# A two-layer decoder trunk: every projection computed token-major, rotation by tokens, turns by DMA, the projections in a new order

## Chip, cores and metric

The kernel runs on one core of one Trainium2 chip. The metric is the device time of one execution in microseconds (us), lower is better: the median of three runs of the kernel before is 318.63 us (317.89 to 319.02). The profile is of one more execution, which took 318.17 us, of which 316.0 us lie between its first and its last instruction (the span).

## What is computed

There are 256 tokens, 1024 features and two layers. A layer normalises `x`, projects it with one weight of 1024 x 4096, and splits the result into eight groups of 512 columns, each of four heads of 128. Four groups (RQ, RK, RV, RZ) feed a retention, four (MQ, MK, MV, MZ) an attention whose 256-token block is its own block, so that it is plain causal attention with a bias table.

```python
h = rms_norm(x, norm_g[i])
rq, rk, rv, rz, mq, mk, mv, mz = jnp.split(h @ w_in[i], cuts, axis=-1)
r_out = retention(rotary(heads(rq)), rotary(heads(rk)), heads(rv), ret_norm_g[i])
r_out = silu(rz) * r_out
m_out = moba(rms_norm(heads(mq), q_g), rms_norm(heads(mk), k_g), heads(mv), rel_bias)
m_out = silu(mz) * m_out
x = x + concatenate([r_out, m_out]) @ w_out[i]
gate = sigmoid(rms_norm(x) @ w_ple_gate[i])
x = x + gate * rms_norm(p[i] @ w_ple[i], ple_norm_g[i])
```

`rotary` turns each pair (x1, x2) of the two halves of a head by an angle that depends on the token. `retention` scores queries against keys, multiplies by a decay table, applies the result to the values, and normalises each head.

## The kernel before

**Weights.** Each group's weight comes in two stages of 1 MB (`wst`, four buffers), each of two pieces of 128 x 1024. ACT rounds a piece to a high part (`wh`, L137) and DVE computes the low part (`wl`, L138), six buffers each, so the pieces of a stage are made at most three stages ahead of TensorE (PE). A product in full precision is three matmuls: high by high, low by high, high by low (`mm3`, L146 to L148).

**Token-major and turned projections.** `project(g)` keeps 128 tokens of the activation stationary and streams 512 weight columns: 8 slices of features x 2 token halves x 3 products, 48 matmuls of 512 columns. The result has tokens on the partitions. MQ, MK, MV, RV and RZ are made this way. MZ, RQ and RK are turned: the weights are stationary and the 256 tokens stream, so that the result has the features of a head on the partitions. `project_turned_pairs` (MZ, L488 to L492) uses 96 matmuls of 256 columns, `project_turned` (RQ, RK, L469 and L470) 32 pairs of one of 512 and one of 256 columns.

**What follows a projection.** MQ and MK are normalised per head (`qk_norm`), repacked by ACT into two planes of 16 bits (`halves`, L255), turned by a DMA on SP's queue (`turned_by_dma`, L262) and copied back to `T` by DVE (L265, two copies for 128 tokens). RQ and RK are already turned: `rope` works on a head at a time, with the halves swapped by two ACT copies (L508, L509) and four DVE instructions (L507, L510, L511, L512), reading cosine and sine rows from `cst`. `gate_turned` needs the tokens' scale as a row, which `spread` and `gather` make by a small DRAM round trip. The attention's scores are made in three pieces (`moba_scores`, L546), each followed later by a softmax on DVE and ACT, a division, and a transpose on PE (`turn`, L250). `moba_out` multiplies turned values with turned probabilities (L586, L587). `ret_scores` (four), `ret_out` (two, L577) and `ret_gate` do the same for retention.

**What sets the order.** PE and SP run in the order in which the code is written; DVE and ACT are ordered by a scheduler, and then each engine works its queue in order. `project` and the turned forms call `tick()` after each sixth matmul or each head, and `later(n, f)` puts `f` into the program n ticks on. So the short groups of matmuls stand between the projections' matmuls at places given by a tick count. `ahead()` puts the next weight load into SP's queue when a stage is used, and DMA turns stand in the same queue where their tick falls. A PE result lies in one of four `acc` buffers (projections) or four `mix` buffers (short groups).

```python
ORDER = (MQ, MK, MV, MZ, RQ, RK, RV, RZ)
later(14, lambda: moba_scores(0, 0, 4))
later(15, lambda: moba_scores(1, 0, 2))
later(16, lambda: moba_scores(1, 2, 2))
project_turned_pairs(MZ, lambda h, ps: gate_turned(MZ, h, ps))
project_turned(RQ, lambda h, ps: rope(RQ, h, ps))
project_turned(RK, lambda h, ps: rope(RK, h, ps))
```

Of the kernel before, what the change touches and what calls it, by code (L numbers as in the profile page):

```python
# [24 lines left out]
H = 4  # L25
# [9 lines left out]
ORDER = (MQ, MK, MV, MZ, RQ, RK, RV, RZ)  # L35
# [6 lines left out]
C_COS, C_SIN = 0, S  # L42
C_DEC = 2 * S
# [12 lines left out]
def tile_hybrid_trunk(ctx: ExitStack, tc: tile.TileContext, first, rest, x, pT, ple_g, rel_bias,  # L56
# [42 lines left out]
    def job(key, fn):  # L99
        jobs.append((key, fn))  # L100
# [80 lines left out]
    cos, sin = cst[:, C_COS:C_COS + S], cst[:, C_SIN:C_SIN + S]  # L181
# [157 lines left out]
    for l in range(DEPTH):  # L339
        for g in ORDER:  # L340
            for half in range(2):
                if l == 0 and g == MQ:
                    first_blocks(half)
                else:
                    stage(("in", l, g, half), w_in[l, g, half])
                if l == 0 and g == RQ and half:
                    job(None, lambda: nc.sync.dma_start(cst, consts))
            if l == 0 and g == MK:
                for m in range(MT):
                    job(None, lambda m=m: nc.sync.dma_start(x_t[:, m], x[:, m]))  # L350
                shifts = bias_table()
            if l == 0 and g == MV:
# [12 lines left out]
    for l in range(DEPTH):  # L365
        rstd, hr, rstd2, epsx = [], [], [], []
        hrs = sm.tile([P, 32], F32, name="hr", bufs=2)
        nc.vector.memset(hrs, 0.0)

        def x_stats():  # L370
            for m in range(MT):
# [12 lines left out]
                h = hrs[:, m:m + 1]  # L384
# [6 lines left out]
            nc.vector.transpose(hrt, hrs)  # L391

        hd = dram.tile([MT, P], F32, name=f"hd{l}")
        hrow = big.tile([P, S], F32, name="hrow", bufs=1)

        hrt = sm.tile([P, 32], F32, name="hrt", bufs=1)

        def spread():

            for m in range(MT):  # L400
                nc.sync.dma_start(hd[m].rearrange("(b i) -> b i", i=32), hrt.rearrange("(b j) i -> b j i", j=32)[:, m])

        def gather():

            nc.sync.dma_start(hrow, bass.AP(tensor=hd.tensor, offset=hd.offset, ap=[[0, P], [1, S]]))
# [51 lines left out]
        def project_turned(g, use):  # L457

            ps = [acc_p.tile([P, 2, S], F32, name="acc") for _ in range(H)]
            for half in range(2):
                parts = load_w(("in", l, g, half))
                for h in range(H):
                    sl = slice(h * DH, (h + 1) * DH)
                    for k in range(4):
                        wh, wl = parts[k // 2]
                        kk, end = half * 4 + k, half == 1 and k == 3
                        nc.tensor.matmul(ps[h], wh[:, k % 2, sl], aB[:, kk], start=kk == 0, stop=False)  # L469
                        nc.tensor.matmul(ps[h][:, 0], wl[:, k % 2, sl], aB[:, kk, 0], start=False, stop=end)  # L470
                    if half:
                        with tc.high_priority(offset=PRIO):
                            use(h, ps[h])
                    tick()

        def project_turned_pairs(g, use):


            ps = [acc_p.tile([P, 2, S], F32, name="acc") for _ in range(H // 2)]
            for half in range(2):  # L480
                parts = load_w(("in", l, g, half))
                for h in range(H):
                    sl = slice(h * DH, (h + 1) * DH)
                    o = ps[h // 2][:, h % 2]
                    for k in range(4):
                        wh, wl = parts[k // 2]
                        kk, end = half * 4 + k, half == 1 and k == 3
                        nc.tensor.matmul(o, wh[:, k % 2, sl], aB[:, kk, 0], start=kk == 0 and h % 2 == 0,  # L488
                                         stop=False, skip_group_check=True)
                        nc.tensor.matmul(o, wh[:, k % 2, sl], aB[:, kk, 1], start=False, stop=False,  # L490
                                         skip_group_check=True)
                        nc.tensor.matmul(o, wl[:, k % 2, sl], aB[:, kk, 0], start=False, stop=end,  # L492
                                         skip_group_check=True)
                    if half and h % 2:
                        with tc.high_priority(offset=PRIO):
                            use(h - 1, ps[h // 2])
                    tick()

        def rope(g, h, ps):
            if h == 0:  # L500
                T[g] = big.tile([P, H, S], F32, name="T")
            dst = T[g][:, h]
            r = DH // 2
            t = tmp_p.tile([P, 2, S], F32, name="tmp")
            b = tmp_p.tile([P, S], F32, name="tmp")
# [20 lines left out]

        def gate_turned(g, h, ps):
            if h == 0:
                G[g] = big.tile([P, H, S], F32, name="G", bufs=1)
            t = tmp_p.tile([P, 2, S], F32, name="tmp")  # L530
            th = tmp_p.tile([P, 2, S], F32, name="tmp")
            nc.vector.tensor_tensor(t, ps, hrow[:, None, :].to_broadcast([P, 2, S]), op=ALU.mult)
            nc.scalar.activation(th, t, AF.Tanh)
            nc.vector.scalar_tensor_tensor(G[g][:, h:h + 2], th, 1.0, t, op0=ALU.add, op1=ALU.mult)
# [3 lines left out]
        def moba_scores(m, h0, per):  # L538
# [17 lines left out]
            ri = sm.tile([P, H], F32, name="ri")  # L556
            nc.vector.reciprocal(ri[:, :per], DEN[m][:, h0:h0 + per])
# [11 lines left out]
            later(8, turn)  # L569

        yT, yTh, yTl, _ = act_tiles()
# [9 lines left out]
        def moba_out(h0):  # L581

            ps = mix_p.tile([P, 2, S], F32, name="mix")
            for j in range(2):
                v = V[MV][:, :, (h0 + j) * DH:(h0 + j + 1) * DH]
                nc.tensor.matmul(ps[:, j], v[:, 0], PT[:, h0 + j, :S], start=True, stop=False)  # L586
                nc.tensor.matmul(ps[:, j, P:], v[:, 1], PT[:, h0 + j, S:], start=False, stop=True)  # L587
# [61 lines left out]
        later(8, spread)  # L649
        later(15, gather)  # L650
# [14 lines left out]
        for h in range(H):  # L665
            later(5 + h, lambda h=h: ret_scores(h))
# [3 lines left out]
        later(3, lambda: ret_out(0))  # L670
        later(4, lambda: ret_out(1))
# [89 lines left out]
def _constants():  # L761
# [6 lines left out]
    c[:, C_COS:C_COS + S] = np.concatenate([cos, cos], 1).T  # L768
    c[:, C_SIN:C_SIN + S] = np.concatenate([-sin, sin], 1).T
# [64 lines left out]
```

## Time and profile before

| | us | |
|---|---|---|
| median of 3 runs | 318.63 | 317.89 to 319.02 |
| the profiled execution | 318.17 | |
| its span | 316.0 | |
| PE busy | 310.0 | 98% |
| DVE busy | 243.3 | 77% |
| ACT busy | 201.0 | 64% |

Matmuls are pipelined, and the profile models their ends: a row gives 0.39 us for a matmul of 512 columns although the next one starts after 0.23 us. So what a matmul costs PE is read from the distance between starts, not from its duration. DVE's and ACT's rows have a similar, smaller overlap: three instructions of 1.22 us each in a row take 3.48 us together, some 0.07 us less than their durations for each. The first layer's eight projections run from 5 us to 123 us, the second's from 166 us to 282 us.

### The profile page before, as it was taken

What the parts mean: (1) busy time and instruction counts of PE and PEld (TensorE: products, weight loads), DVE (VectorE), ACT (ScalarE), POOL (GpSimd) and SP (SyncE); (2) the same over time, 40 slices, a digit from 0 to 9 for tenths busy, and PEclk for the clock granted to TensorE, in tenths of its full rate; (3) what the DMA queues carried; (4) which work ended last, traced back from release to release, by engine and by line L of the source; (5) the groups of instructions that cost most, each with busy time, mean ns of one, the idle gap of its engine ahead of it and who ended that gap; (6) DMA issues with size and microseconds to landing.
All of it is one profiled execution on the core that took longest, in us unless ns stands there. A gap on an engine that the chain in (4) does not pass through costs nothing.

```text
span 316.0 us, 4502 instructions
## 1 busy us (share of the span) xinstructions
PE 310.0 (98%) x1609; PEld 263.2 (83%) x1609; DVE 243.3 (77%) x444; ACT 201.0 (64%) x382; POOL 27.5 (9%) x45
## 2 busy tenths in 40 slices
PE   8999999999999999999999999999999999999994
PEld 4888899888888888888888888998888888888884
DVE  5798889679967977959698877586799669969632
ACT  5888947886842635845586987469769435547411
POOL 4015200000001100011001521000000011000000
PEclk9999999999999999999999999999999999999999
DMA  7999999444560139500997459943345530390001
GB/s 263 418 409 395 243 276 421 163 152 152 222 234 1 33 64 427 242 2 34 385 418 251 177 127 308 372 144 133 133 141 197 196 135 17 63 386 2 33 33 66
DMA packets 23350, 62.17 MB, mean 197 GB/s; under 512 B 13853, under 2 KB 14881, under 8 KB 17185
## 3 DMA queue, kind: packets, MB, share of 16 engines
q1 hardware_dynamic: 23320, 61.89, 55.5%
q8 instruction: 12, 0.20, 0.3%
q14 instruction: 10, 0.07, 0.1%
q10 hardware_dynamic: 8, 0.00, 0.0%
HBM read 57.69 MB, written 1.06 MB: 186 GB/s over the span
## 4 chain that ended last, share of the span: by engine, by line
PE 94%; ACT 2%; DVE 1%; issue 1%
PE acc L146 21%; PE acc L147 21%; PE acc L148 21%; PE acc L469 8%; PE acc L470 4%; PE acc L492 2%; PE acc L490 2%; PE acc L488 2%; PE mix L250 2%; PE mix L577 2%; PE mix L546 2%; PE mix L169 1%; PE mix L146 1%; PE mix L147 1%; PE mix L148 1%
## 5 line engine op out<-in xcount | busy, mean ns | idle before, releaser
L138 DVE TENSOR_TENSOR wl<-wst,wh 128x1024 fp32r<-128x1024 f32 x96 | 115.6, 1219 | 24.4 <-ACT wh L137 23.7
L137 ACT CAST wh<-wst 128x1024 fp32r<-128x1024 f32 x96 | 98.4, 1053 | 41.9 <-PE acc L148 25.0
L146 PE MATMUL acc<-wh,a 128*128 128x512 f32 (+1 forms) x296 | 116.2, 392 | 0.0
L148 PE MATMUL acc<-wh,a 128*128 128x512 f32 (+1 forms) x296 | 113.8, 384 | 0.0
L147 PE MATMUL acc<-wl,a 128*128 128x512 f32 (+1 forms) x296 | 113.7, 384 | 0.0
L148 PEld LDWEIGHTS acc<-wh,a 128*128 128x128 f32 x296 | 55.6, 188 | 11.2
L147 PEld LDWEIGHTS acc<-wl,a 128*128 128x128 f32 x296 | 55.7, 188 | 11.0 <-DVE wl L243 0.6
L146 PEld LDWEIGHTS acc<-wh,a 128*128 128x128 f32 x296 | 55.8, 188 | 10.7 <-ACT wh L236 0.4
L469 PE MATMUL acc<-a,wh 128*128 128x512 f32 x128 | 46.8, 407 | 0.6 <-DVE tmp L507 0.6
L470 PE MATMUL acc<-a,wl 128*128 128x256 f32 x128 | 35.9, 281 | 0.0
L469 PEld LDWEIGHTS acc<-a,wh 128*128 128x128 f32 x128 | 24.1, 188 | 6.3 <-PE mix L587 0.9
L470 PEld LDWEIGHTS acc<-a,wl 128*128 128x128 f32 x128 | 24.2, 189 | 0.1
L488 PE MATMUL acc<-a,wh 128*128 128x256 f32 x64 | 18.6, 291 | 0.0
L729 ACT ACTIVATE tmp<-acc,hr 128x512 f32<-128x512 f32 (+1 forms) x9 | 5.8, 640 | 19.4 <-PE acc L148 17.7
L492 PE MATMUL acc<-a,wl 128*128 128x256 f32 x64 | 18.1, 283 | 0.0
L490 PE MATMUL acc<-a,wh 128*128 128x256 f32 x64 | 18.1, 283 | 0.0
L159 POOL TENSOR_TENSOR ro<-rs_t,neghalf 128x4 f32<-128x4 f32 x4 | 4.0, 1006 | 142.3 <-DVE rs_t L158 142.3
L730 DVE SCALAR_TENSOR_TENSOR tmp<-tmp,E 128x512 f32<-128x512 f32 (+1 forms) x9 | 5.7, 631 | 12.7 <-ACT tmp L729 12.7
L255 ACT COPY u<-tok 128x1024 uint16<-128x1024 uint16 x12 | 12.6, 1062 | 0.3 <-DVE tok L451 0.3
L488 PEld LDWEIGHTS acc<-a,wh 128*128 128x128 f32 x64 | 12.3, 192 | 0.1
L490 PEld LDWEIGHTS acc<-a,wh 128*128 128x128 f32 x64 | 12.3, 192 | 0.1
L492 PEld LDWEIGHTS acc<-a,wl 128*128 128x128 f32 x64 | 12.2, 191 | 0.0
(121 smaller groups left out, 373.1 us busy)
## 6 DMA issues: line engine op xcount, KB each, us to landing
wst<-in_w_in SPq DMA_DIRECT2D x30, 1024.0 KB, 6.2
wst<-in_w_out SPq DMA_DIRECT2D x8, 1024.0 KB, 4.8
wst<-in_w_gate SPq DMA_DIRECT2D x8, 1024.0 KB, 6.6
wst<-in_w_ple SPq DMA_DIRECT2D x2, 1024.0 KB, 6.5
wst<-in_rest SPq DMA_DIRECT2D x4, 384.0 KB, 7.2
E<-in_rest SPq DMA_DIRECT2D x3, 384.0 KB, 3.8
x_t<-in_x SPq DMA_DIRECT2D x2, 512.0 KB
gb<-in_ple_g SPq DMA_DIRECT2D x2, 512.0 KB, 4.5
```

Of the source, the lines that this page charges most:

```text
L137: nc.scalar.copy(hi, s)
L138: nc.vector.tensor_tensor(lo, s, hi.bitcast(F32), op=ALU.subtract)
L146: nc.tensor.matmul(ps, ah[:, k], wh[:, kk], start=start, stop=False)
L147: nc.tensor.matmul(ps, ah[:, k], wl[:, kk], start=False, stop=False)
L148: nc.tensor.matmul(ps, al[:, k], wh[:, kk], start=False, stop=stop)
L250: nc.tensor.transpose(ps[:, j * P:(j + 1) * P], src[:, b * P:(b + 1) * P], ident)
L255: nc.scalar.copy(u, src.bitcast(U16).rearrange("p (n t) -> p t n", t=2))
L469: nc.tensor.matmul(ps[h], wh[:, k % 2, sl], aB[:, kk], start=kk == 0, stop=False)
L470: nc.tensor.matmul(ps[h][:, 0], wl[:, k % 2, sl], aB[:, kk, 0], start=False, stop=end)
L488: nc.tensor.matmul(o, wh[:, k % 2, sl], aB[:, kk, 0], start=kk == 0 and h % 2 == 0, stop=False, skip_group_check=True)
L490: nc.tensor.matmul(o, wh[:, k % 2, sl], aB[:, kk, 1], start=False, stop=False, skip_group_check=True)
L492: nc.tensor.matmul(o, wl[:, k % 2, sl], aB[:, kk, 0], start=False, stop=end, skip_group_check=True)
```

## The change

All eight groups use `project`, so `project_turned`, `project_turned_pairs`, `gate_turned` and the DRAM round trip go. RQ and RK are rotated with the tokens on the partitions, and their four pieces per layer then go the way of MQ and MK: repacked by ACT, turned by DMA, copied by DVE. The attention's output is made with the tokens on the partitions, divided and gated in one pass, and turned by DMA too. The order of the projections is MQ, MK, RQ, RK, MZ, MV, RV, RZ. The three scores, the three transposes, the two halves of `moba_out`, the four `ret_scores` and the two `ret_out` each stand in one place.

```diff
-ORDER = (MQ, MK, MV, MZ, RQ, RK, RV, RZ)
+ORDER = (MQ, MK, RQ, RK, MZ, MV, RV, RZ)
...
                 if l == 0 and g == RQ and half:
-                    job(None, lambda: nc.sync.dma_start(cst, consts))
+                    job(None, lambda: nc.sync.dma_start(cst[:, :C_DEC], consts[:, :C_DEC]))
+                if l == 0 and g == MZ and half:
+                    job(None, lambda: nc.sync.dma_start(cst[:, C_DEC:], consts[:, C_DEC:]))
...
-        def rope(g, h, ps):
...
-            nc.scalar.copy(b, ps[:, 1])
-            nc.vector.tensor_tensor(t[:, 0], ps[:, 0], b, op=ALU.add)
-            nc.scalar.copy(b[:r], t[r:, 0])
-            nc.scalar.copy(b[r:], t[:r, 0])
-            nc.vector.tensor_tensor(t[:, 1], t[:, 0], cos, op=ALU.mult)
-            nc.vector.tensor_tensor(b, b, sin, op=ALU.mult)
-            nc.vector.tensor_tensor(dst, t[:, 1], b, op=ALU.add)
+        def rope(g, ps):
+            for m in range(MT):
+                src = ps[m].rearrange("p (h a d) -> p h a d", h=H, a=2)
...
+                nc.vector.tensor_tensor(tv, src, cos, op=ALU.mult)
+                nc.vector.tensor_tensor(bv, src[:, :, ::-1], sin, op=ALU.mult)
+                o = tok_p.tile([P, GW], F32, name="tok")
+                nc.vector.tensor_tensor(o, t, b, op=ALU.add)
+                u = halves(o)
+                later((9 if g == RQ else 4) + m, lambda m=m, u=u: to_heads(g, m, u))
...
-            def divide():
-                for j in range(per):
-                    nc.scalar.activation(sv[:, j], sv[:, j], AF.Copy, scale=ri[:, j:j + 1])
-            later(3, divide, 0)
...
-            later(8, turn)
+            later(7, turn)
...
-        def moba_out(h0):
...
-            y = tok_p.tile([P, 2, S], F32, name="tok")
-            nc.vector.tensor_tensor(y, ps, G[MZ][:, h0:h0 + 2], op=ALU.mult)
-            hi = yTh[:, H + h0:H + h0 + 2]
-            nc.scalar.copy(hi, y)
-            nc.vector.tensor_tensor(yTl[:, H + h0:H + h0 + 2], y, hi.bitcast(F32), op=ALU.subtract)
+        def moba_out(m):
+            ps = pv(m, lambda h, m, b: PT[:, h, (m + b) * P:(m + b + 1) * P], V[MV])
+            ri = sm.tile([P, H], F32, name="ri")
+            nc.vector.reciprocal(ri, DEN[m])
+            nc.vector.tensor_scalar(ri, ri, hr[m], None, op0=ALU.mult)
+            y = tok_p.tile([P, GW], F32, name="tok")
+            for h in range(H):
+                sl = slice(h * DH, (h + 1) * DH)
+                nc.vector.scalar_tensor_tensor(y[:, sl], ps[:, sl], ri[:, h:h + 1], G[MZ][:, m, sl],
+                                               op0=ALU.mult, op1=ALU.mult)
+            u = halves(y)
+            later(3 + m, lambda: parts_by_dma(yT[m], H, u))
...
-        later(14, lambda: moba_scores(0, 0, 4))
-        later(15, lambda: moba_scores(1, 0, 2))
-        later(16, lambda: moba_scores(1, 2, 2))
+        def scores():
+            moba_scores(0, 0, 4)
+            moba_scores(1, 0, 2)
+            moba_scores(1, 2, 2)
+        later(16, scores)
+        for g in (RQ, RK):
+            ps = project(g)
+            with tc.high_priority(offset=PRIO):
+                rope(g, ps)
+        ps = project(MZ)
+        with tc.high_priority(offset=PRIO):
+            gate(MZ, ps)
         ps = project(MV)
         with tc.high_priority(offset=PRIO):
             value(MV, ps)
-        project_turned_pairs(MZ, lambda h, ps: gate_turned(MZ, h, ps))
-        later(10, lambda: moba_out(0))
-        later(11, lambda: moba_out(2))
-        project_turned(RQ, lambda h, ps: rope(RQ, h, ps))
-        project_turned(RK, lambda h, ps: rope(RK, h, ps))
-        for h in range(H):
-            later(5 + h, lambda h=h: ret_scores(h))
+        later(3, lambda: [moba_out(m) for m in range(MT)])
+        later(5, lambda: [ret_scores(h) for h in range(H)])
         ps = project(RV)
         with tc.high_priority(offset=PRIO):
             value(RV, ps)
-        later(3, lambda: ret_out(0))
-        later(4, lambda: ret_out(1))
+        later(3, lambda: [ret_out(m) for m in range(MT)])
```

Three places show how the queues change. The first is DVE in layer 0, from the last rows before the third projection's end to the first score. Before (`w_435` and `w_446` are the turned queries of MQ, `w_493` and `w_503` the turned keys of MK, `L550` adds the bias to a score):

```order
L138 TENSOR_TENSOR wl<-wst,wh 128x1024 x3
L265 COPY T<-w_435 128x4x128 x2
L138 TENSOR_TENSOR wl<-wst,wh 128x1024
L265 COPY T<-w_446 128x4x128 x2
L138 TENSOR_TENSOR wl<-wst,wh 128x1024
L265 COPY T<-w_493 128x4x128 x2
L265 COPY T<-w_503 128x4x128 x2
```

After, `w_430` and `w_441` are the queries, `w_487` and `w_497` the keys, and L452, L453 and L455 the rotation of RQ:

```order
L452 TENSOR_TENSOR tmp<-acc,cst 128x512
L453 TENSOR_TENSOR tmp<-acc,cst 128x512
L265 COPY T<-w_430 128x4x128 x2
L138 TENSOR_TENSOR wl<-wst,wh 128x1024
L452 TENSOR_TENSOR tmp<-acc,cst 128x512
L453 TENSOR_TENSOR tmp<-acc,cst 128x512
L265 COPY T<-w_441 128x4x128 x2
L455 TENSOR_TENSOR tok<-tmp 128x512
L138 TENSOR_TENSOR wl<-wst,wh 128x1024
L455 TENSOR_TENSOR tok<-tmp 128x512
L265 COPY T<-w_487 128x4x128 x2
L138 TENSOR_TENSOR wl<-wst,wh 128x1024 x2
```

(The keys' second half, `w_497`, follows, and then the rotation of RK.) The copies of the queries and keys now stand behind and between the six instructions that rotate RQ, which wait for RQ's last matmuls.

The second place is SP's queue from the middle of layer 0's projections on. Before, behind the turned keys of MK (`w_493`, `w_503`), only loads stand there:

```order
L405 DMA hrow<-hd_141 128x256
L262 DMA_TRANSPOSE w_493<-u_400 128x8x128
L262 DMA_TRANSPOSE w_503<-u_414 128x8x128
L347 DMA cst<-in_consts 128x1536
L125 DMA wst<-in_w_in 128x2048 x6
L125 DMA wst<-in_w_out 128x2048 x4
L330 DMA pf<-in_pT 128x512
```

After, `u_507` and `u_515` are the repacked RQ, `u_627` and `u_635` RK, `u_866` and `u_885` the attention's output; the loads on both sides of `w_703` are those of RV's second stage and of RZ:

```order
L349 DMA cst<-in_consts 128x1024
L125 DMA wst<-in_w_in 128x2048 x3
L262 DMA_TRANSPOSE w_656<-u_507 128x8x128
L262 DMA_TRANSPOSE w_666<-u_515 128x8x128
L262 DMA_TRANSPOSE w_683<-u_627 128x8x128
L125 DMA wst<-in_w_in 128x2048
L262 DMA_TRANSPOSE w_703<-u_635 128x8x128
L125 DMA wst<-in_w_in 128x2048 x2
L125 DMA wst<-in_w_out 128x2048 x2
L262 DMA_TRANSPOSE w_937<-u_866 128x8x128
L262 DMA_TRANSPOSE w_950<-u_885 128x8x128
L125 DMA wst<-in_w_out 128x2048 x2
```

Six turns now stand among the weight loads, and a load behind a turn is issued only when ACT has made what the turn reads.

The third place is ACT in layer 1 of the changed kernel, at the end of MV (`u_2124` is the second half of RK, `L462` makes the values, `u_2355` and `u_2374` are the attention's output):

```order
L255 COPY u_2124<-tok 128x1024
L137 CAST wh<-wst 128x1024 x3
L462 ACTIVATE V<-acc,rstd 128x512 x2
L137 CAST wh<-wst 128x1024 x2
L255 COPY u_2355<-tok 128x1024
L255 COPY u_2374<-tok 128x1024
```

The third of the three casts ahead of the values is the first piece of RZ's weight, so the values stand behind that weight's load.

## Rows read from the trace of the kernel before

**Rows 1.** The page: busy time by engine, and the granted clock by slice.
```profile
PE 310.0 (98%) x1609; PEld 263.2 (83%) x1609; DVE 243.3 (77%) x444; ACT 201.0 (64%) x382; POOL 27.5 (9%) x45
...
PEclk9999999999999999999999999999999999999999
```

**Rows 2.** The page: the chain that ended last, by engine.
```profile
PE 94%; ACT 2%; DVE 1%; issue 1%
```

**Rows 3.** Timeline of PE: start, duration, instruction; MZ's, RQ's and RZ's projections.
```profile
38.22 0.28 PE L488 MATMUL acc<-a,wh 128*128 128x256 f32 x1
...
46.86 1.06 PE L546 MATMUL mix<-T 128*128 128x128 f32 x8
...
52.70 0.39 PE L469 MATMUL acc<-a,wh 128*128 128x512 f32 x1
...
58.71 0.40 PE L469 MATMUL acc<-a,wh 128*128 128x512 f32 x1
...
101.10 0.48 PE L146 MATMUL acc<-wh,a 128*128 128x512 f32 x1
...
122.96 0.27 PE L250 MATMUL mix<-ident,x_t 128*128 128x128 f32 x1
```

**Rows 4.** Timeline of PE: where it waits, in brackets what it waited for.
```profile
68.86 0.39 PE L587 MATMUL mix<-PS,V 128*128 128x128 f32 x2
69.54 0.47 PE L469 MATMUL acc<-a,wh 128*128 128x512 f32 x1 [0.29 <-DVE tmp L507]
```

**Rows 5.** Timeline of PE: short groups and the projection's matmuls behind them.
```profile
67.78 0.59 PE L586 MATMUL mix<-PS,V 128*128 128x256 f32 x2
68.20 0.39 PE L587 MATMUL mix<-PS,V 128*128 128x128 f32 x2
...
97.13 1.05 PE L577 MATMUL mix<-V,PS 128*128 128x128 f32 x8
97.94 0.48 PE L146 MATMUL acc<-wh,a 128*128 128x512 f32 x1
98.25 0.40 PE L147 MATMUL acc<-wl,a 128*128 128x512 f32 x1
...
99.40 1.95 PE L577 MATMUL mix<-V,PS 128*128 128x128 f32 x16
```

**Rows 6.** Groups by line and shape: count | busy us, mean ns | idle before, releaser.
```profile
L138 DVE TENSOR_TENSOR wl<-wst,wh 128x1024 fp32r<-128x1024 f32 x96 | 115.6, 1219 | 24.4 <-ACT wh L137 23.7
L137 ACT CAST wh<-wst 128x1024 fp32r<-128x1024 f32 x96 | 98.4, 1053 | 41.9 <-PE acc L148 25.0 <-DMA wst<-in_w_in 3.5 <-issue 3.3
L255 ACT COPY u<-tok 128x1024 uint16<-128x1024 uint16 x12 | 12.6, 1062 | 0.3 <-DVE tok L451 0.3
L512 DVE TENSOR_TENSOR T<-tmp 128x256 f32<-128x256 f32 x16 | 6.6, 421 | 0.3
L265 DVE COPY T<-w 128x512 uint16<-128x512 uint16 x16 | 6.4, 458 | 2.4 <-DMA w<-u 2.4
L451 DVE TENSOR_TENSOR tok<-acc,qr 128x512 f32<-128x512 f32 x8 | 5.5, 687 | 2.7 <-POOL qr L449 2.7
L517 ACT ACTIVATE V<-acc,rstd 128x512 f32<-128x512 f32 x8 | 5.5, 688 | 5.8 <-PE acc L148 5.7
L627 DVE TENSOR_SCALAR T<-mix,bmv,ro 128x128 f32<-128x128 f32 x16 | 5.4, 400 | 0.0
L554 ACT ACTIVATE tok<-tok,nm 128x256 f32<-128x256 f32 x8 | 4.0, 501 | 0.0
```

**Rows 7.** Timeline of DVE, layer 0, before the third projection's end.
```profile
34.63 3.48 DVE L138 TENSOR_TENSOR wl<-wst,wh 128x1024 fp32r<-128x1024 f32 x3
```

**Rows 8.** DMA turns (issue ns min/median/max, and us to landing) and weight loads.
```profile
L262 SPq DMA_TRANSPOSE w<-u x12: 1232/1246/4650, 28.4 to 273.6; - x12
...
DMA to landing us min/median/max: 3.0/3.1/6.7
...
wst<-in_w_in SPq DMA_DIRECT2D x30, 1024.0 KB, 6.2
```

More of the change, by code (lines that the diff above doesn't have):

```diff
@@ L40 @@
 LATE = 5
-C_COS, C_SIN = 0, S
-C_DEC = 2 * S
+C_ROT = 0
+C_DEC = MT * 2 * DH
 C_END = C_DEC + H * 256
@@ L179, in tile_hybrid_trunk @@
     qkg = cp.tile([P, DEPTH], F32, name="qkg")
-    cos, sin = cst[:, C_COS:C_COS + S], cst[:, C_SIN:C_SIN + S]
+    rot = cst[:, C_ROT:C_DEC].rearrange("p (m t d) -> p m t d", m=MT, t=2)
     dec = cst[:, C_DEC:C_END].rearrange("p (h n) -> p h n", h=H)
@@ L351, in tile_hybrid_trunk @@
                 shifts = bias_table()
-            if l == 0 and g == MV:
+            if l == 0 and g == RQ:
                 job(None, lambda: nc.sync.dma_start(tbias, shifts))
@@ L366, in tile_hybrid_trunk @@
         rstd, hr, rstd2, epsx = [], [], [], []
-        hrs = sm.tile([P, 32], F32, name="hr", bufs=2)
-        nc.vector.memset(hrs, 0.0)
         def x_stats():
@@ L383, in x_stats @@
                 rsqrt(r, ss, 1.0 / D)
-                h = hrs[:, m:m + 1]
+                h = sm.tile([P, 1], F32, name="hr", bufs=4)
                 nc.vector.tensor_scalar(h, r, 0.5, None, op0=ALU.mult)
@@ L390, in x_stats @@
                 rstd2.append(r2)
[L391 to L405, printed above, removed]
         T, V, G = {}, {}, {}
@@ L455, in qk_norm @@
                 later(7 + m, lambda m=m, u=u: to_heads(g, m, u, qkg[:, l:l + 1] if g == MQ else None))
[L457 to L463, printed above, removed]
-                for h in range(H):
[L465 to L497, printed above, removed]
@@ L499, in rope @@
-        def rope(g, h, ps):
[L500 to L505, printed above, removed]
-            nc.scalar.copy(b, ps[:, 1])
-            nc.vector.tensor_tensor(t[:, 0], ps[:, 0], b, op=ALU.add)
-            nc.scalar.copy(b[:r], t[r:, 0])
-            nc.scalar.copy(b[r:], t[:r, 0])
-            nc.vector.tensor_tensor(t[:, 1], t[:, 0], cos, op=ALU.mult)
-            nc.vector.tensor_tensor(b, b, sin, op=ALU.mult)
-            nc.vector.tensor_tensor(dst, t[:, 1], b, op=ALU.add)
+        def rope(g, ps):
+            for m in range(MT):
+                src = ps[m].rearrange("p (h a d) -> p h a d", h=H, a=2)
+                t = tmp_p.tile([P, GW], F32, name="tmp")
+                b = tmp_p.tile([P, GW], F32, name="tmp")
+                tv, bv = (v.rearrange("p (h a d) -> p h a d", h=H, a=2) for v in (t, b))
+                cos, sin = (rot[:, m, j].rearrange("p (a d) -> p a d", a=2)[:, None].to_broadcast([P, H, 2, DH // 2])
+                            for j in range(2))
+                nc.vector.tensor_tensor(tv, src, cos, op=ALU.mult)
[4 more added lines that the diff above has]
+                later((9 if g == RQ else 4) + m, lambda m=m, u=u: to_heads(g, m, u))
@@ L525, in gate @@
                 nc.vector.scalar_tensor_tensor(G[g][:, m], th, 1.0, ps[m], op0=ALU.add, op1=ALU.mult)
[L527 to L534, printed above, removed]
         PT, DEN = big.tile([P, H, S + P], F32, name="PS", bufs=1), {}
@@ L555, in moba_scores @@
                                      accum_out=DEN[m][:, h0 + j:h0 + j + 1])
-            ri = sm.tile([P, H], F32, name="ri")
-            nc.vector.reciprocal(ri[:, :per], DEN[m][:, h0:h0 + per])
-            def divide():
-                for j in range(per):
-                    nc.scalar.activation(sv[:, j], sv[:, j], AF.Copy, scale=ri[:, j:j + 1])
-            later(3, divide, 0)
             def turn():
@@ L568, in turn @@
                 nc.scalar.copy(PT[:, h0:h0 + per, m * P:m * P + n], pt.rearrange("p (h t) -> p h t", h=per))
-            later(8, turn)
-        yT, yTh, yTl, _ = act_tiles()
+            later(7, turn)
+        yT = act_tiles()[0]
         def pv(m, lhs, v):
@@ L579, in pv @@
             return ps
-        def moba_out(h0):
[L583 to L587, printed above, removed]
-            y = tok_p.tile([P, 2, S], F32, name="tok")
-            nc.vector.tensor_tensor(y, ps, G[MZ][:, h0:h0 + 2], op=ALU.mult)
-            hi = yTh[:, H + h0:H + h0 + 2]
-            nc.scalar.copy(hi, y)
-            nc.vector.tensor_tensor(yTl[:, H + h0:H + h0 + 2], y, hi.bitcast(F32), op=ALU.subtract)
+        def moba_out(m):
[10 more added lines that the diff above has]
+            later(3 + m, lambda: parts_by_dma(yT[m], H, u))
         ST = {}
@@ L648, in tile_hybrid_trunk @@
             tick_now()
-        later(8, spread)
-        later(15, gather)
         ps = project(MK)
@@ L659, in tile_hybrid_trunk @@
             value(MV, ps)
-        project_turned_pairs(MZ, lambda h, ps: gate_turned(MZ, h, ps))
-        later(10, lambda: moba_out(0))
-        later(11, lambda: moba_out(2))
-        project_turned(RQ, lambda h, ps: rope(RQ, h, ps))
-        project_turned(RK, lambda h, ps: rope(RK, h, ps))
-        for h in range(H):
-            later(5 + h, lambda h=h: ret_scores(h))
+        later(3, lambda: [moba_out(m) for m in range(MT)])
+        later(5, lambda: [ret_scores(h) for h in range(H)])
         ps = project(RV)
@@ L767, in _constants @@
     cos, sin = np.cos(ang).astype(f), np.sin(ang).astype(f)
-    c[:, C_COS:C_COS + S] = np.concatenate([cos, cos], 1).T
-    c[:, C_SIN:C_SIN + S] = np.concatenate([-sin, sin], 1).T
+    rot = np.stack([np.concatenate([cos, cos], 1), np.concatenate([-sin, sin], 1)], 1)
+    c[:, C_ROT:C_DEC] = rot.reshape(MT, P, 2 * DH).transpose(1, 0, 2).reshape(P, -1)
     rel = np.arange(S)[None, :] - np.arange(P)[:, None]
```

## Prediction

> **What bounds the kernel now.** I read the page's busy times first: PE is busy for 310.0 of 316.0 us, DVE for 243.3, ACT for 201.0, and PE's granted clock is full in all forty slices [rows 1]. A busy PE alone proves little, since its ends are modelled, so the chain that ended last is next: PE holds 94% of it [rows 2]. Then I read the starts of PE's matmuls one after the other. They follow each other without a hole but for a few places, the largest in the middle of the kernel being one before RK's projection (below). So the kernel is as long as PE's instruction stream. A change helps if it shortens that stream and DVE, ACT and SP still deliver in time.
>
> **What the change takes out of the stream.** From starts [rows 3]: MZ's first 72 matmuls of 256 columns take 46.86 - 38.22 = 8.64 us, 0.120 each. RQ's 17 pairs take 58.71 - 52.70 = 6.01 us, 0.3535 a pair. RZ, token-major, and the 48 matmuls of 512 columns behind it take 122.96 - 101.10 = 21.86 us for 96, 0.2277 each. The streamed columns are the same in all three forms; the turned ones cost more because they need more matmuls.
>
> - MZ: 96 x 0.120 = 11.52 us becomes 48 x 0.2277 = 10.93.
> - RQ and RK: 64 x 0.3535 = 22.62 us becomes 96 x 0.2277 = 21.86.
> - Together 1.35 us less per layer.
>
> On the fixed price of a matmul: two of 256 columns cost 0.240 us and one of 512 costs 0.228, so a matmul fewer saves 0.012 us [rows 3], and 48 + 32 = 80 fewer would by that alone save 1.0 of the 1.35. The Trainium skill ("TensorE: Matmul & The Clock Gate", section "Wait — 56ns, not 53.3ns?") states a smaller fixed price, about 2.5 ns per matmul. By that figure an estimate is 80 x 2.5 ns = 0.2 us per layer instead of 1.35. The trace disagrees for these matmuls, and the sum goes by the trace.
>
> **A wait that goes.** RK's turned projection waits for a PSUM buffer that RQ's rotation still reads: 0.68 us pass between two starts [rows 4] where a pair of 128 columns takes about 0.23 (two of the records below). That is 0.45 us per layer. In the new form the buffer wanted next was left a whole projection earlier, so this wait goes.
>
> **Short groups.** Scores, transposes, retention scores and outputs keep their matmuls. The attention's output has four pairs now, 0.42 + 0.23 us each [rows 4, 5], 2.60 in all, and 24 records of 128 columns after. Eight such records take 97.94 - 97.13 = 0.81 us, and the matmul behind them loses 0.08 (0.31 to the next start instead of 0.23): 0.111 each. Sixteen take 101.10 - 99.40 = 1.70 and the same 0.08: again 0.111 [rows 3, 5]. So 24 cost 2.67, 0.07 more than before. The same two groups say that a group has no price of its own beyond its records, so laying short groups in one place saves PE nothing. If the 0.08 were a fixed price after all, nine groups fewer would give 0.7 us per layer; I take 0 and keep it as a low end.
>
> Sum on PE: 1.35 + 0.45 - 0.07 = 1.73 us per layer, 3.5 in all.
>
> **What the other engines pay.** DVE loses 32 rotation instructions of 0.42 us (13.5) and eight passes of 128x512 in the gate and the attention's output (5.5 at 0.69). It gets twelve rotation passes (8.3), twelve copies behind six new turns (5.5), four passes (2.8) and eight of 128x128, at most 0.40 each (3.2) [rows 6]. That is 19.8 against 19.0 us per layer, next to 158 us of PE. Strided and reversed PSUM reads of the rotation have no row; L451 reads PSUM with a broadcast operand at 0.69, and I take that. At twice, the four rotation passes of a group would add 2.8 us, which matters in the next paragraph. ACT gets six repackings of 1.06 us and loses 24 half-partition copies and eight divisions, the latter alone about as long as L554's 0.50 each; it comes out with less to do. So no engine becomes the bound by its total, and what can cost time is a single late delivery. I followed four.
>
> *Scores, layer 0.* All starts below take off 0.07 us per DVE instruction for overlap. DVE was through with its three casts at 34.63 + 3.48 = 38.1 [rows 7], and the third projection's end is PE's 38.22 [rows 3], RQ's end in the new order. From there DVE has six passes of 0.69, eight copies of 0.46 and four casts of 1.22 before the last key copy: 12.7 - 18 x 0.07 = 11.4 us, to 49.5. PE reaches the scores after RK, 38.22 + 10.93 = 49.15. I take 0.4 us of waiting. Low end 0; high end 3.2, with the rotation passes at twice. In layer 1 the key copies stand ahead of RQ's rotation, and I take 0.
>
> *Probabilities.* From RK's end R, DVE has four rotation passes, three bias passes, three maxima and two casts: 6.9 + 2.4 - 0.8 = 8.5 us; the first maximum is out 1.2 us earlier, at R + 7.3. ACT then needs eight exponentials of at most 0.50 and one cast, to R + 12.4. PE's third transpose stands behind the scores (16 records, 2.6), seven ticks of six matmuls (9.6) and eight transposes (0.9), at R + 13.1. So 0 us, with 0.7 us of room.
>
> *Attention's output.* It needs MV's values, three ticks into RV: R + 2.6 + 10.9 + 1.3 + 10.9 = R + 25.7 is MV's end, so R + 29.8. This is where SP's queue matters. RK's repacking follows the transposes and comes at about R + 15.5. The load of RV's second stage goes out behind that turn at R + 17, and RZ's first behind the next at R + 20. At 6.2 us a load [rows 8] it lands at R + 26.2. In layer 1 ACT casts RZ's first piece (1.05) ahead of the values (0.69): R + 27.9, 1.9 us in time. 0 us, and this is the place that could cost most.
>
> *Retention.* DVE waits for the turned attention's output ahead of the retention's decay passes. PE ends the attention's output at R + 32.5; the gating passes end 1.5 us later, repacking 1.1, turn 3.1 [rows 8], then about 6 us of DVE: R + 44.2, against R + 46 where `ret_out` stands. 0 us, or 1.8 with the longest turn, 6.7.
>
> So -3.5 + 0.4 = -3.1 us on the profiled execution's 318.17: 315.1. It lies 0.5 below the median of the runs, so the median to expect is 315.5 us. What lies around the span does not change.
>
> **Rivals.**
> 1. *Part is lost to late deliveries.* A wait of about 0.8 us per layer at the scores or the probabilities. For it: room of 0.7 us at one and none at the other. Against it: in the second layer the copies come early. 315.5 + 1.6 = 317.1 us.
> 2. *Nothing is left.* Either the rotation reads PSUM at twice the price (3.2 at the scores), or the gain per matmul is no more than a fixed price far below 0.012. At a quarter of it, 0.003, 80 fewer matmuls give 0.24, with the wait gone and the dearer output 0.62 per layer, 1.2 in all, less 0.4: 317.8. The figure of the Trainium skill cited above would give about this. Against it: the durations come from the same operand sizes in the same kernel. About 318.
> 3. *Slower, by SP's queue.* Turn issues took 1.25 us, but one took 4.65 [rows 8]. If both of RK's turns issue that slowly, RZ's load is out 6.8 us later. It decides from 1.9 us of delay on: the values are then late, PE stands at the attention's output, and everything behind it moves. 6.8 - 1.9 = 4.9 us in layer 1 alone: 320.4. For it: the weights behind a turn have no way around it, and six turns are new. Against it: by then no load is in flight, since SP has stood at the turn, and the median issue is 1.25.
>
> **Chances.** Forecast 0.61, first rival 0.16, second 0.13, third 0.10. A change under 0.3%, about 1 us, is what a measurement of this kernel cannot tell from none. The forecast and the first rival are faster (0.77), the second the same (0.13), the third slower (0.10). The forecast alone spans 314.3 (no wait at the scores, a little from grouping) to 316.4. For eight in ten the range runs to 318.4, which leaves out the third rival and takes in most of the second.
>
> **What will show it.** Right: MZ, RQ and RK as 48 matmuls each at 0.228 us from start to start; no wait before RK; MQ's end to RV's start shorter by 1.7 us in each layer; PE still above 97%. Wrong: PE waiting before the first score for the copies (more than 1 us), at the transposes for exponentials, or at the attention's output for the values, with SP standing at RK's turns while RZ's load lands late; or DVE's rotation passes far from 0.69 us.

## The result, and the profile after

The kernel after takes 314.53 us, median of four runs (314.51 to 314.63), next to 318.40 for the kernel before on the same chip (317.89 to 319.02, now four runs as well): a ratio of 0.9878, 95% interval 0.9859 to 0.9897. The forecast was 315.5, with 314.3 as its own low end and 318.4 as the upper end for eight in ten. The profiled execution took 314.63 us, with a span of 312.5 (before 318.17 and 316.0), so the traces have to explain 3.5 us.

The page of the kernel after: busy time by engine, the granted clock, and the engines' shares of the chain that ended last.

```profile
PE 307.1 (98%) x1465; PEld 255.8 (82%) x1465; DVE 241.4 (77%) x434; ACT 190.6 (61%) x330; POOL 27.4 (9%) x45
...
PEclk9999999999999999999999999999999999999998
...
PE 97%; DMA 1%; DVE 1%; ACT 0%; issue 0%
```

Against [rows 1, 2] PE has 144 fewer matmuls and 2.9 us less to do, and holds 97% of the chain instead of 94%. The chain's 2% of ACT and 1% without a releaser are gone, and 1% of DMA is new. The kernel is still as long as PE's instruction stream.

Next the timeline of PE in the kernel after: start, duration, instruction. L482 are the scores, L250 the transposes of the probabilities, L506 the outputs of attention (79.43, 236.75), L528 and L529 the retention scores (from 84.84 on). 4.89 is the first matmul of the projections, and 38.71 RK's first. The row at 121.45 stands where 122.96 stands in [rows 3], and the last one at the same place a layer on.

```profile
4.89 0.80 PE L146 MATMUL acc<-wh,a 128*128 128x512 f32 x1
...
38.48 0.39 PE L148 MATMUL acc<-wh,a 128*128 128x512 f32 x1
38.71 0.39 PE L146 MATMUL acc<-wh,a 128*128 128x512 f32 x1
...
49.59 2.78 PE L482 MATMUL mix<-T 128*128 128x128 f32 x16
52.02 0.58 PE L146 MATMUL acc<-wh,a 128*128 128x512 f32 x1
...
61.74 1.47 PE L250 MATMUL mix<-ident,tok 128*128 128x128 f32 x12
62.97 0.48 PE L146 MATMUL acc<-wh,a 128*128 128x512 f32 x1
...
79.43 2.84 PE L506 MATMUL mix<-V,PS 128*128 128x128 f32 x24
82.02 0.48 PE L146 MATMUL acc<-wh,a 128*128 128x512 f32 x1
...
84.84 0.59 PE L528 MATMUL mix<-T 128*128 128x256 f32 x2
...
87.23 0.39 PE L529 MATMUL mix<-T 128*128 128x128 f32 x2
87.38 0.48 PE L146 MATMUL acc<-wh,a 128*128 128x512 f32 x1
...
121.45 0.60 PE L250 MATMUL mix<-ident,x_t 128*128 128x128 f32 x4
...
164.64 0.48 PE L146 MATMUL acc<-wh,a 128*128 128x512 f32 x1
...
236.75 2.84 PE L506 MATMUL mix<-V,PS 128*128 128x128 f32 x24
...
278.78 0.60 PE L250 MATMUL mix<-ident,x_t 128*128 128x128 f32 x4
```

No row carries a wait, nor does any other PE row from the first projection to the end. RK's 48 matmuls take 49.59 - 38.71 = 10.88 us, 0.2267 each, and RK's first stands 0.23 behind its predecessor where the turned one stood 0.68 behind [rows 4]. The ends of the same stretches in the kernel before (layer 0's second end is the 122.96 of [rows 3]):

```profile
4.74 0.91 PE L146 MATMUL acc<-wh,a 128*128 128x512 f32 x1
...
166.14 0.48 PE L146 MATMUL acc<-wh,a 128*128 128x512 f32 x1
...
282.23 0.49 PE L250 MATMUL mix<-ident,x_t 128*128 128x128 f32 x3
```

So layer 1's stretch shrank from 116.09 to 114.14 us, by 1.95. Layer 0's shrank from 118.22 to 116.56, by 1.66 only, since its first three projections, the same 144 matmuls in both kernels, took 33.82 us (4.89 to 38.71) where they had taken 33.48 (4.74 to 38.22). That is lost among the first four matmuls (the fourth stands at 6.72, 1.83 us behind the first, where it stood at 6.20, 1.46 behind); the trace shows no wait there, and the cause stays open. PE also starts 0.15 later. 1.95 + 1.66 - 0.15 is 3.46 of the 3.5 us.

The other engines deliver in time, with little to spare. DVE at the end of the third projection, up to the last copy of the keys:

```profile
38.23 0.69 DVE L452 TENSOR_TENSOR tmp<-acc,cst 128x512 f32<-128x512 f32 x1 [0.62 <-PE acc L148]
...
48.40 0.79 DVE L265 COPY T<-w 128x512 uint16<-128x512 uint16 x2
```

The copies end at 49.19 us, 0.4 before PE reaches the scores. ACT in layer 0 (the last exponential of the probabilities, and a cast that waits for its load) and in layer 1 (RZ's first weight, then the attention's values):

```profile
60.36 0.49 ACT L490 ACTIVATE tok<-tok,nm 128x256 f32<-128x256 f32 x1
...
72.26 2.00 ACT L137 CAST wh<-wst 128x1024 fp32r<-128x1024 f32 x2 [4.33 <-DMA wst<-in_w_in]
...
233.38 1.05 ACT L137 CAST wh<-wst 128x1024 fp32r<-128x1024 f32 x1 [2.84 <-DMA wst<-in_w_in]
234.34 1.26 ACT L462 ACTIVATE V<-acc,rstd 128x512 f32<-128x512 f32 x2
```

The exponentials are through at 60.85, 0.9 us before the first transposes; the last of them are read by the third four transposes, at 62.62, so the room is 1.8 us. The values are through at 235.6, 1.1 us before the attention's output at 236.75, although the cast in front of them waited 2.84 us for its load. SP shows why that load, RZ's first, was late: in layer 1 SP stood at RQ's and RK's turns for 20.58 us and let nothing past, and RZ's loads stand behind one more turn, at 226.60.

```profile
202.43 20.58 SPq L262 DMA_TRANSPOSE w<-u  x3
...
225.31 1.24 SPq L262 DMA_TRANSPOSE w<-u  x1
226.60 1.09 SPq L125 DMA_DIRECT2D wst<-in_w_in  x2
```

### The profile page after: what moved, and what is told of

Read it like the earlier page. It is cut to its first block, busy times and chain, and to the rows that moved or that the text cites. A ratio compares the mean times of both kernels' runs of the same rounds, so it can differ in the third digit from the quotient of the medians.

```text
span 312.5 us, 4188 instructions
## 1 busy us (share of the span) xinstructions
PE 307.1 (98%) x1465; PEld 255.8 (82%) x1465; DVE 241.4 (77%) x434; ACT 190.6 (61%) x330; POOL 27.4 (9%) x45
## 4 chain that ended last, share of the span: by engine, by line
PE 97%; DMA 1%; DVE 1%; ACT 0%; issue 0%
PE acc L147 28%; PE acc L148 28%; PE acc L146 28%; PE mix L506 3%; PE mix L250 3%; PE mix L482 2%; PE mix L146 1%; PE mix L147 1%; PE mix L148 1%; DMA E<-in_first 1%; PE mix L528 1%; PE mix L529 1%; DVE wl L243 0%; DVE a L241 0%; ACT tmp L660 0%; DVE tmp L661 0%
## 5 line engine op out<-in xcount | busy, mean ns | idle before, releaser
L146 PE MATMUL acc<-wh,a 128*128 128x512 f32 (+1 forms) x392 | 153.3, 391 | 0.0
L147 PE MATMUL acc<-wl,a 128*128 128x512 f32 (+1 forms) x392 | 151.3, 386 | 0.1
L148 PE MATMUL acc<-wh,a 128*128 128x512 f32 (+1 forms) x392 | 151.2, 386 | 0.0
L146 PEld LDWEIGHTS acc<-wh,a 128*128 128x128 f32 x392 | 73.9, 189 | 14.7 <-ACT wh L236 0.6
L148 PEld LDWEIGHTS acc<-wh,a 128*128 128x128 f32 x392 | 73.8, 188 | 14.9
L147 PEld LDWEIGHTS acc<-wl,a 128*128 128x128 f32 x392 | 73.8, 188 | 14.7 <-DVE wl L243 0.6
L255 ACT COPY u<-tok 128x1024 uint16<-128x1024 uint16 x24 | 25.2, 1056 | 7.8 <-DVE tok L518 5.5
L265 DVE COPY T<-w 128x512 uint16<-128x512 uint16 x32 | 12.9, 454 | 8.9 <-DMA w<-u 8.9
L506 PEld LDWEIGHTS mix<-V,PS 128*128 128x128 f32 x96 | 11.3, 192 | 0.3
L506 PE MATMUL mix<-V,PS 128*128 128x128 f32 x96 | 11.4, 275 | 0.0
L434 POOL TENSOR_TENSOR qr<-qms,neghalf 128x4 f32<-128x4 f32 x8 | 10.0, 1263 | 13.5 <-DVE qms L432 10.5
L429 ACT ACTIVATE tmp<-acc 128x128 f32<-128x128 f32 x32 | 8.4, 289 | 1.4 <-PE acc L148 1.4
## 6 DMA issues: line engine op xcount, KB each, us to landing
x_t<-in_x SPq DMA_DIRECT2D x2, 512.0 KB, 11.3
```

What stands on the lines that cost most here:

```text
L146: nc.tensor.matmul(ps, ah[:, k], wh[:, kk], start=start, stop=False)
L147: nc.tensor.matmul(ps, ah[:, k], wl[:, kk], start=False, stop=False)
L148: nc.tensor.matmul(ps, al[:, k], wh[:, kk], start=False, stop=stop)
L255: nc.scalar.copy(u, src.bitcast(U16).rearrange("p (n t) -> p t n", t=2))
L265: nc.vector.tensor_copy(raw[:, t], w[:, t])
L429: nc.scalar.activation(junk[:, sl], ps[m][:, sl], AF.Square, accum_out=ss[:, h:h + 1])
```

## Experiments

Each is the kernel after with one thing changed, unless it says otherwise.

**What a matmul costs by itself.** MZ, RQ and RK stay token-major, but each of their matmuls of 512 columns is split into two of 256: 288 matmuls more, the same columns, the same order of everything else.

```diff
-                    mm3(ps[m], aT[m], half * 4 + k, parts[k // 2], k % 2, ...)
+                    for c in range(2):
+                        cs = slice(c * 256, c * 256 + 256)
+                        nc.tensor.matmul(ps[m][:, cs], ah[:, kk], wh[:, k % 2, cs], ...)
+                        nc.tensor.matmul(ps[m][:, cs], ah[:, kk], wl[:, k % 2, cs], ...)
+                        nc.tensor.matmul(ps[m][:, cs], al[:, kk], wh[:, k % 2, cs], ...)
```

> The changed kernel, with each matmul of 512 columns in MZ, RQ and RK done as two of 256 columns with the same weights: 144 more matmuls per layer, the same columns, the same short groups and order. Theory (a matmul has a fixed price of 0.012 us on PE, from 2 x 0.120 - 0.228 in the kernel before, and that made most of the gain): 288 x 0.0123 = 3.5 us more, 318.0 us. Rival (the fixed price is small, 2.5 ns, and the gain came from elsewhere): 0.7 us more, 315.2 us.

Measured: 318.57 us, the same as the kernel before (ratio 1.0004, 0.9995 to 1.0014). The 84 matmuls between scores and transposes on PE:

```profile
53.38 0.47 PE L411 MATMUL acc<-wh,a 128*128 128x256 f32 x1
...
63.64 1.47 PE L250 MATMUL mix<-ident,tok 128*128 128x128 f32 x12
```

They take 10.26 us where 42 of twice the size took 61.74 - 52.02 = 9.72: 0.0129 us for each matmul more. 288 of them are 3.7 of the 4.04 us lost. The theory holds: a matmul has a price of its own, and it is the prediction's 0.012. The run adds 288 matmuls, though, and the change takes only 80 per layer out of the three projections. At 0.0129 that is 1.03 of the 1.50 us per layer that the forms turn out to be worth (below). Most of the other 0.47 lies in RQ's and RK's turned pairs: a pair took 0.3535 us where one matmul of 512 columns and one of 256, each among its like, come to 0.2267 + 0.120, and 64 x 0.0068 is 0.44. No run shows why a pair costs more.

**Short groups apart.** Scores, attention output, retention scores and retention output stand at ticks of their own again, nine groups more per layer.

```diff
-        later(16, scores)
+        later(16, lambda: moba_scores(0, 0, 4))
+        later(17, lambda: moba_scores(1, 0, 2))
+        later(18, lambda: moba_scores(1, 2, 2))
...
-        later(3, lambda: [moba_out(m) for m in range(MT)])
-        later(5, lambda: [ret_scores(h) for h in range(H)])
+        for m in range(MT):
+            later(3 + m, lambda m=m: moba_out(m))
+        for h in range(H):
+            later(5 + h, lambda h=h: ret_scores(h))
```

> The changed kernel with its short groups apart again: scores at ticks 16, 17, 18, transposes seven ticks behind each, the two halves of the attention's output at 3 and 4, retention scores at 5 to 8, the two outputs at 3 and 4; 14 groups per layer instead of 5. Theory (a short group has no price beyond its records): no difference, 314.5 us within 0.4. Rival (each group costs a restart of 0.08 us, so laying them together gave part of the gain): 18 x 0.08 = 1.4 us more, 315.9 us.

Measured: 315.99 us, 1.5 above the kernel after, so the theory's "no difference" is missed. It is the rival's number, but the trace gives it another cause. Layer 1's stretch grew by 0.25 us; in layer 0 the third transposes, behind scores that now end two ticks later, wait for the exponentials:

```profile
66.43 0.93 PE L250 MATMUL mix<-ident,tok 128*128 128x128 f32 x4 [0.38 <-ACT tok L490]
```

From RK's first matmul to its end layer 0 takes 83.85 us (39.11 to 122.96) where the kernel after takes 82.74 (38.71 to 121.45): 1.1 more, about 0.25 as in layer 1 and 0.9 around this wait. The remaining 0.4 of 1.7 us of span is RK starting at 39.11, after waits in the first projection. Since the total mixed these, it was run again with the transposes one tick later (`later(8, turn)`).

> The short groups stand apart as in e2_apart, but the probabilities' transposes run one tick later (8 for 7), so that they need not wait for the exponentials of scores that moved later. Theory (a short group costs about 0.03 us where it stands; e2_apart's loss was the wait for exponentials in layer 0 and the start): 315.0 us, and the wait of about 0.9 us ahead of layer 0's last transposes is gone. Rival (each of the 18 more places costs about 0.08 us): 315.9 us, as e2_apart.

Measured: 314.91 us (314.55 to 315.52; ratio 0.9884, 0.9869 to 0.9899), 0.4 above the kernel after, and the wait is gone. PE in layer 1, with the scores in three places:

```profile
164.65 0.48 PE L146 MATMUL acc<-wh,a 128*128 128x512 f32 x1
...
206.92 1.05 PE L482 MATMUL mix<-T 128*128 128x128 f32 x8
207.73 0.48 PE L146 MATMUL acc<-wh,a 128*128 128x512 f32 x1
...
209.19 1.02 PE L482 MATMUL mix<-T 128*128 128x256 f32 x4
...
279.03 0.60 PE L250 MATMUL mix<-ident,x_t 128*128 128x128 f32 x4
```

The six matmuls behind the first group take 209.19 - 207.73 = 1.46 us, 0.10 more than six at 0.2267; the last record of a group gives most of that back by being short. The layer is 114.38 us against 114.14: 0.24 for nine groups, 0.03 each. So among token-major matmuls a group has a small price of its own.

**Scores two ticks earlier.** The change's own safety: how late do the keys' copies come?

```diff
-        later(16, scores)
+        later(14, scores)
```

(The transposes go to `later(9)`, so that they stay where they were.)

> The changed kernel with the three scores two ticks earlier, at tick 14 (their transposes stay at the same tick). Theory (in layer 0 the key copies end just before the scores, at 49.2 us, because DVE takes them behind RQ's rotation): PE reaches the scores at 46.9 and waits 2.4 us; in layer 1 the copies are done long before, 0. So 316.9 us, with one PE wait of about 2.4 us at the first score of layer 0. Rival (the copies have room, or the place of the scores does not matter): 314.5 us.

Measured: 316.67 us (ratio 0.9943, 0.9929 to 0.9957). PE in layer 0:

```profile
46.94 1.05 PE L482 MATMUL mix<-T 128*128 128x128 f32 x8
49.67 1.97 PE L482 MATMUL mix<-T 128*128 128x256 f32 x8 [1.68 <-DVE T L265]
51.29 0.58 PE L146 MATMUL acc<-wh,a 128*128 128x512 f32 x1
```

The scores take 4.35 us instead of 2.43, and the wait names the key copies. Nothing waits in layer 1, where the copies are early, as the prediction had it. The scores' tick 16 leaves about 0.4 us of room, and not more.

**The old order of projections with everything else new.**

```diff
-ORDER = (MQ, MK, RQ, RK, MZ, MV, RV, RZ)
+ORDER = (MQ, MK, MV, MZ, RQ, RK, RV, RZ)
```

(The calls move with it, the attention's output goes to tick 10 behind MZ, and the bias table's load goes with MV.)

> The changed kernel with the projections in the old order MQ, MK, MV, MZ, RQ, RK, RV, RZ; all token-major, the attention's output at tick 10 behind MZ, everything else as in the changed kernel. Theory (PE's own work is the same; the order is there to give RK time to be rotated, repacked, turned and copied before the retention scores at tick 5 of RV): rotation with its casts about 9 us behind RK's end, repacking 1, turn 3.2, copies 0.8, about 14 us against 6.8 us, so PE waits some 7 us in each layer: about 329 us (325 to 332). Rival (the order itself gives nothing and costs nothing): 314.5 us.

Measured: 338.56 us (ratio 1.0631, 1.0600 to 1.0663): the direction of the theory, with 24.0 us lost where it had 14.5. PE at the retention scores of layer 0 and layer 1, up to the first matmul behind them; then a stretch of PE's time (us, PE busy, PEld, DVE, ACT, POOL, granted clock, DMA share, GB/s):

```profile
90.15 1.22 PE L528 MATMUL mix<-T 128*128 128x256 f32 x2 [5.36 <-DVE T L265]
94.41 0.80 PE L529 MATMUL mix<-T 128*128 128x128 f32 x2 [3.04 <-DVE T L265]
...
98.01 0.47 PE L146 MATMUL acc<-wh,a 128*128 128x512 f32 x1
...
259.12 1.22 PE L528 MATMUL mix<-T 128*128 128x256 f32 x2 [5.93 <-DVE T L265]
263.41 0.80 PE L529 MATMUL mix<-T 128*128 128x128 f32 x2 [3.07 <-DVE T L265]
...
267.70 0.60 PE L146 MATMUL acc<-wh,a 128*128 128x512 f32 x1
```

```profile
94.00:97.00 3.00, 2.59 (x8) 2.32 (x9) 1.46 (x6) 0.00 (x0) 0.00 (x0) 0.50 0.99 401
```

RK's projection now stands directly ahead of RV's, and its turned keys come 8.4 us late. With layer 1's two waits (5.93 and 3.07) these are 17.4 of 23.1 us of span; the forecast had 14. What it left out altogether is the clock: behind the waits PE works at a granted clock of 0.50, the lower of its two levels (1.2 GHz). Without the wait inside them layer 0's four retention scores take 98.01 - 90.15 - 3.04 = 4.82 us and layer 1's 5.51, where the kernel after takes 87.38 - 84.84 = 2.54. That is 5.3 of the other 5.7 us. All token-major in the old order loses 20 us against the kernel before, five times what the whole change gains.

**RK's turns ahead of the loads (the third rival's mechanism, aimed at).** SP stands at both of RK's turns before it issues the loads of RV's second stage and of RZ.

```diff
-                later((9 if g == RQ else 4) + m, lambda m=m, u=u: to_heads(g, m, u))
+                later((9 if g == RQ else 1) + m, lambda m=m, u=u: to_heads(g, m, u))
```

> RK's turns are issued at ticks 1 to 3 after their stage for 4 to 6, ahead of the loads of retention's weights in SP's queue, which then start 1 to 2 us later. Theory (there is room of 1.1 to 1.9 us between the last projected attention values and the attention output): at most 0.5 us, 314.5 to 315.0 us. Rival (the third of the prediction: SP's queue decides, and a delayed load of weights stops TensorE): 317 us and more, with a wait for weights in RV or RZ.

Measured: 314.69 us (ratio 0.9875, 0.9862 to 0.9889), the kernel after within its scatter. ACT in layer 0, and then PE:

```profile
75.53 2.00 ACT L137 CAST wh<-wst 128x1024 fp32r<-128x1024 f32 x2 [7.50 <-DMA wst<-in_w_in]
77.43 1.26 ACT L462 ACTIVATE V<-acc,rstd 128x512 f32<-128x512 f32 x2
```

```profile
79.50 2.73 PE L506 MATMUL mix<-V,PS 128*128 128x128 f32 x23
```

The delay is real: the cast waits 7.5 us for its load, and starts 3.3 us later than in the kernel after (72.26). But values are through at 78.7, and PE wants them at 79.50. The queue's delay was absorbed with 0.8 us left here, and 1.0 in layer 1 (values through at 235.8, PE at 236.82). So the way from a late load to the values exists; the rival's own case, both turns issuing slowly and RZ's load 6.8 us late, did not come up in any run.

**The next step in the same direction.** If PE's stream is the length, more of it can go. The probabilities' twelve transposes per layer become DMA turns (six `DMA_TRANSPOSE` in all) and twelve copies on DVE, and RK's turns go back to tick 9.

```diff
+            u = halves(s)
-                pt = mix_p.tile([P, 512], F32, name="mix")
-                transposed(s, range(4), pt)
-                nc.scalar.copy(PT[:, h0:h0 + per, m * P:m * P + n], pt...)
-            later(7, turn)
+                w = tok_p.tile([P, 2, 4, P], U16, name="w16", bufs=2)
+                nc.sync.dma_start(w..., u..., transpose=True)
+                for t in range(2):
+                    nc.vector.tensor_copy(raw[:, t, h0:h0 + per, m * P:m * P + n], w[:, t]...)
+            later(PTD, turn)
```

> The twelve transposes of the probabilities per layer leave TensorE; the probabilities turn by DMA and two VectorE copies per stage, and RK's turns start five ticks later to leave SP's queue to them. Theory (TensorE is the bound, and DMA turns cost nothing while they land in time): 24 transposes at 0.11 us go, 2.6 us, so 311.9 us. Rival (SP's queue and VectorE's copies are at their limit: more turns deliver retention's keys or the probabilities late): nothing is left or it is slower, 314.5 us and above, with a wait of TensorE in front of the attention output or of the retention scores.

Measured: 312.40 us (311.55 to 312.69; ratio 0.9795, 0.9780 to 0.9811), faster than both. The page, and PE's ends of layer 1:

```profile
PE 304.7 (98%) x1441; PEld 253.2 (82%) x1441; DVE 244.9 (79%) x446; ACT 193.0 (62%) x330; POOL 28.5 (9%) x45
```

```profile
163.67 0.48 PE L147 MATMUL acc<-wh,a 128*128 128x512 f32 x1
...
276.47 0.60 PE L251 MATMUL mix<-ident,x_t 128*128 128x128 f32 x4
```

The layer is 112.80 us, 1.34 less than after, which is the 1.23 of the transposes and the 0.1 lost behind them. Layer 0, from RK's first matmul on, gives 1.36; the total is 2.1 and not 2.7 because RK starts 0.4 us later in this run. No PE row of the two stretches waits behind the first projection, so DVE's 3.5 us more cost nothing.

## Why the prediction was right, step by step

- *PE's stream is the length.* Right, from both sides: work added to PE lengthened the kernel (first experiment), and work taken away shortened each layer by its own length (the last).
- *1.35 us per layer from the forms.* Right in kind, somewhat small. 144 matmuls at 0.2267 are 32.64 us against 11.52 + 22.62 = 34.14: 1.50. The 0.2277 that I read [rows 3] is a mean over 96 with one restart behind a group in it, and the 0.08 of that restart was already in the price of the short group's records. It was counted twice. How much of the 1.50 is the number of matmuls stands with the first experiment: 1.03.
- *0.012 us per matmul, against the figure of a page.* The experiment gives 0.0129, measured with nothing else changed. The Trainium skill ("TensorE: Matmul & The Clock Gate", section "Wait — 56ns, not 53.3ns?") states about 2.5 ns per matmul; an estimate by that figure for 288 matmuls is 0.7 us, and 4.04 were measured. For these matmuls the measurement decides.
- *0.45 us for the wait before RK.* Small by 0.08: I set the gap of 0.68 [rows 4] against a pair inside a group, but the last pair of a group is followed after 0.15 (87.38 - 87.23). 0.68 - 0.15 = 0.53.
- *Attention's output 0.07 dearer.* Right: 2.59 us and the 0.08 behind, forecast 2.67.
- Together 1.50 + 0.53 - 0.07 = 1.96 per layer; layer 1 shows 1.95.
- *Grouping is worth nothing.* Right for this change, not in general. Between two wholly token-major kernels it is worth 0.24 us per layer. From before to after it is not: taking each group of layer 1 from its first start to the seventh projection matmul behind it, less six at their usual price, the scores cost 2.61 before and 2.63 after, the transposes 1.30 and 1.34, the retention scores 2.70 and 2.63, the retention outputs 2.70 and 2.69. Together that is 9.31 and 9.29. Behind scores and transposes the turned matmuls lost less than token-major ones do (2.68 and 1.39 with the same groups apart in the token-major kernel), and so there was little to save.
- *0.4 us of waiting at the scores.* This step failed, by little: 0. The rotation passes are as assumed, but DVE's chain is 10.96 us long (38.23 to 49.19) for 11.4, since its instructions overlap by about 0.10 us each where I took off 0.07. And it begins 0.48 ahead of RK's first matmul, when the first half of RQ's tokens is done, where I had 0.1. PE's late start has no part in this, since the chain waits for RQ's matmuls and moves with them. Two ticks earlier the wait is there.
- *The other deliveries cost 0.* Right, though the room was not where I put it. The values, with R = 206.93 in layer 1, come at R + 28.7 for R + 27.9: RZ's cast starts at R + 26.4 for R + 26.2, and behind it I counted 0.69 for the values where their two passes take 1.26. The probabilities were early: the exponentials end at R + 11.3 in layer 0 (R = 49.59) for R + 12.4. Retention's decay passes end at R + 42.7 in layer 1 for R + 44.2. DVE's total fell by 1.9 us (243.3 to 241.4) where I had 1.6 more, which costs nothing either way.

In sum, against the forecast of -3.1 us: 0.4 for the wait that did not come, twice 0.23 for the two small terms, less 0.5 lost at the start, makes -3.5. The start's 0.5 us had no term in the prediction. How much of it the change brings is open: RK's first matmul, at 38.71 here, stands between 38.48 and 39.13 in the five other runs with the same code up to there (all but the split matmuls and the old order). That the total came within 0.4 us is partly luck, since misses of 0.9 one way met 0.5 the other way.

Of the rivals, the first (part lost to late deliveries) has its two places, with 0.4 and 1.8 us of room; PE waited at the first when the scores came two ticks earlier, and at the second when they were spread over two ticks more. The second fell with the first experiment (0.0129 a matmul) and with the rotation's passes at 0.68. Of the third, a later load was absorbed with 0.8 us left; its slow turns did not come: RK's turns issued in 1.23 to 1.29 us in that run and in the kernel after.

## What to carry to other kernels

When one engine's stream is the length of the kernel, count its instructions from start to start, and take their price from a row of equal ones with no short group among them. Then the question for every edit is only whether the others still deliver in time, and the answer is a place in the order: a turn by DMA cost PE nothing where its use stood a projection or more away, and over 8 us a layer where it did not. Two edits that look independent (another form of a projection, another order) may need each other: here the form without the order lost 20 us. The order without the form was not run.

## What the hardware showed that was not expected

- The slowest DMA turns were slower than before, the usual ones were not. The kernel after has 24 instead of 12 [rows 8]; the medians are 1.24 us to issue and 3.2 to landing, for 1.25 and 3.1, but the longest issue is 5.5 us for 4.65 and the longest landing 11.7 for 6.7. The two longest issues (5.5 and 5.1) are layer 0's RQ turns, straight behind three weight loads; whether those loads make them slow is not shown.

```profile
L262 SPq DMA_TRANSPOSE w<-u x24: 1232/1244/5473, 28.9 to 268.2; - x24
...
DMA to landing us min/median/max: 3.0/3.2/11.7
```

- Reading PSUM with the two halves of a head swapped and a broadcast table costs DVE what a pass over plain SBUF operands costs (L455):

```profile
L452 DVE TENSOR_TENSOR tmp<-acc,cst 128x512 f32<-128x512 f32 x8 | 5.5, 683 | 0.6 <-PE acc L148 0.6
L453 DVE TENSOR_TENSOR tmp<-acc,cst 128x512 f32<-128x512 f32 x8 | 5.4, 678 | 0.0
L455 DVE TENSOR_TENSOR tok<-tmp 128x512 f32<-128x512 f32 x8 | 5.3, 684 | 1.7 <-PE mix L250 1.7
```

- After waits of 5.36 and 3.04 us PE came back at a granted clock of 0.50, so a late delivery cost more than its own length: in the old order 17.4 us of waits made the span 23.1 longer.
